# Grouped heads' outputs added on chip, queries stored by halves from ScalarE's queue, latent heads stored by token tiles, in a two-layer grid encoder

## The chip, the cores and the metric

The kernel runs on one core of a Trainium2 chip. The metric is the device time of one execution in microseconds; the time given for a kernel is the median of its runs.

## What is computed

Two request groups, 512 and 256 tokens of width 1024, go through the same two layers and are handled as 768 tokens side by side. Each layer is half an FFN (SwiGLU, inner width 2752), a mixer, half an FFN, with an RMS norm ahead of each. All arithmetic is float32; the kernel gets it from a faster matmul type by splitting operands in a high and a low part and adding the products.

```python
# even layer: the mixer of two head groups
qa, ka, va, cq, ckv, kr = jnp.split(h @ w_in, splits, axis=-1)
oa = _neighbourhood_attention(heads(qa), heads(ka), heads(va), na_bias)   # 8 heads of 64
ob = _mla(cq, ckv, kr, q_norm, w_uq, kv_norm, w_ukv, cos, sin)            # 8 latent heads, 64 + 32
x = x + jnp.concatenate([oa, ob], axis=-1) @ w_out
# odd layer: the grouped mixer, 16 query heads on 4 key/value heads of 64
q = _apply_rope(_rmsnorm(q.reshape(b, n, GQA_HEADS, HEAD_DIM), q_norm), cos, sin)
k = _apply_rope(_rmsnorm(k.reshape(b, n, GQA_KV_HEADS, HEAD_DIM), k_norm), cos, sin)
p = softmax(q k / 8);  o = p v;  x = x + o @ w_out
```

## The kernel before

Features stand on the 128 partitions and tokens along the free axis: `x` is 8 tiles of 128 x 768. Six stages follow one another: FFN, mixer `mixer_ab`, FFN, FFN, mixer `mixer_gqa`, FFN. Inside the FFN stages the order of instructions is the written one (`manual_schedule`); in the mixers the framework's planner places the instructions of each engine by its own estimate of a timeline, under the dependences of tiles and a few added by hand (`anchor`). Each engine, and each DMA queue (SP's and ACT's), then works through its own list in order.

**Attention, shared by both mixers (`attention`, from L1028 on).** A list of heads is worked off in steps. `s_step` makes scores on TensorE (L1079), takes the row maximum on DVE (L1090) and the exponential with its row sum on ACT (L1098); `norm` (L1062, L1065) divides by the sum on DVE and POOL. `t_step` transposes the probabilities on TensorE (L1117) and splits them in a high part `pth` on ACT (L1123) and a low part `ptl` on DVE (L1124). `v_step` multiplies by the values (L1138, L1139); the stationary operand holds the high part of 64 value columns beside their low part, so the output `o` has 128 rows of which the upper and the lower 64 must still be added. `leave` takes `o` out of PSUM, first the 256 tokens of the second group, later the 512 of the first. Between steps, `fill.advance` runs pieces of the projections (`proj`, L944 to L948) and their transposes as filler for TensorE. `poll` is called after each step and moves finished heads on.

**Taking the outputs out.** In `mixer_ab` (`late` false), `leave` copies one half of `o` by ACT (L1162) to `of`, moved to the partitions of the other half, and DVE adds the two (L1163) into `osum`, which holds a pair of heads on 128 partitions. In `mixer_gqa` (`late` true), `leave` copies all 128 rows to `of`, on DVE for 256 tokens (L1160) and on ACT for 512 (L1158), and SP stores them (L1166) in the DRAM scratch `oscr`, where the two halves of a head land as two parts of the same 64 rows.

**From there to the output projection (`out_operand`).** The output projection wants each pair of heads as a high and a low part in the tile `o` (`self.o`). With `bounce` false (`mixer_ab`), `begin` takes the finished `osum` to `split2`: a cast on ACT (L1496) and a subtraction on POOL (L1497); when the filler is not yet over and the tile `o` has no room, `osum` is stored (L1471) and later loaded (L1517). With `bounce` true (`mixer_gqa`), `begin` loads both parts of a pair by SP (L1477); four polls later `split` adds them on POOL (L1484; at the tail on DVE), casts on ACT (L1486, or L1489 while `o` has no room) and subtracts on POOL (L1487, L1490); in the second case the result goes to DRAM (L1491) and comes back later (L1515).

**The grouped queries.** `post_qk` normalizes and rotates four query heads for a pair of token tiles; `later_q` transposes them in two halves of four 128 x 128 blocks (L1865), ACT copies each half into its part of the staging tile `stage` (L1867, one buffer), and SP stores the whole (L1871, 512 KB) in `gq`. A head loads its queries from there (L1893).

**The latent heads.** In `mixer_ab`, `chunk` projects queries and keys of four latent heads for one token tile; `later` transposes them and stages queries (w = 0) and keys (w = 1) apart in `mst` (three buffers), copied half by ACT (L1655) and half by DVE (L1657). SP stores each `mst` (L1659) in `mq`, laid out as 96 rows x (w, head, high/low, 768 tokens). A head reads its 1152 KB from there (L1728; L1550 for the first head), and `kk` and `q` are slices along tokens.

Of the kernel before, what the change touches and what calls it, by code (L numbers as in the profile page):

```python
# [15 lines left out]
P = 128  # L16
# [119 lines left out]
class Kernel:  # L136
# [891 lines left out]
    def attention(self, heads, fill, rate, poll, lead=6, pbufs=9, late=False, start_fill=1400):  # L1028
# [119 lines left out]
        def leave(h, o, moves):  # L1148
# [3 lines left out]
            if not late and k not in sums:  # L1152
                sums[k] = pool.tile([P, T], F32, tag="osum", name="osum", bufs=2)
            for dst, src, w in moves:
                c, sc = slice(dst, dst + w), slice(src, src + w)
                if late:
                    if w > NS:
                        nc.scalar.copy(out=of[:, c], in_=o[:, sc])  # L1158
                    else:
                        nc.vector.tensor_copy(out=of[:, c], in_=o[:, sc])  # L1160
                else:
                    nc.scalar.copy(out=of[mine, c], in_=o[its, sc])  # L1162
                    nc.vector.tensor_tensor(out=sums[k][mine, c], in0=o[mine, sc], in1=of[mine, c], op=ALU.add)  # L1163
            if late:
                a, b = min(m[0] for m in moves), max(m[0] + m[2] for m in moves)
                nc.sync.dma_start(out=self.oscr[k][mine].rearrange("r part t -> part r t")[:, :, a:b], in_=of[:, a:b])  # L1166
# [292 lines left out]
    def out_operand(self, fill, order, bufs, bounce=True):  # L1459
# [5 lines left out]
        S.pool, S.done, S.todo, S.split, S.late, S.polls = None, set(), list(order), deque(), deque(), 0  # L1465

        def begin(k):
            if not bounce:
                t = self.sums.pop(k)
                if S.pool is None:  # L1470
                    nc.sync.dma_start(out=self.oscr[k][:, 0], in_=t)  # L1471
                    S.late.append(k)
                else:
                    split2(k, t)
                return
            t = self.ap_.tile([P, 2, T], F32, tag="osum", name="osum", bufs=bufs)
            nc.sync.dma_start(out=t, in_=self.oscr[k])  # L1477
            S.split.append((S.polls, k, t))

        def split(tail=False):  # L1480
            _, k, t = S.split.popleft()
            eng = nc.vector if tail else nc.gpsimd
            s, r = t[:, 0], t[:, 1]
            eng.tensor_tensor(out=s, in0=s, in1=r, op=ALU.add)  # L1484
            if S.pool is not None:
                nc.scalar.copy(out=self.o[:, k, 1], in_=s)  # L1486
                eng.tensor_tensor(out=self.o[:, k, 0], in0=s, in1=f32(self.o[:, k, 1]), op=ALU.subtract)  # L1487
                return
            nc.scalar.copy(out=r.bitcast(F32R), in_=s)  # L1489
            eng.tensor_tensor(out=s.bitcast(F32R), in0=s, in1=r, op=ALU.subtract)  # L1490
            nc.sync.dma_start(out=self.oscr[k], in_=t)  # L1491
            S.late.append(k)

        def split2(k, t):
# [4 lines left out]
        def poll(slot):  # L1499
# [3 lines left out]
            S.polls += 1  # L1503
            if S.split and S.polls - S.split[0][0] >= 4:
                split()
            elif len(S.split) < bufs and S.todo and {2 * S.todo[0], 2 * S.todo[0] + 1} <= S.done:
                begin(S.todo.pop(0))
# [4 lines left out]
            if S.pool is not None and S.late:  # L1512
                k = S.late.popleft()
                if bounce:
                    nc.sync.dma_start(out=f32(self.o[:, k]), in_=self.oscr[k])  # L1515
                elif k >= 0:
                    nc.sync.dma_start(out=f32(self.o[:, k, 0]), in_=self.oscr[k][:, 0])  # L1517
                    S.late.append(-1 - k)
                else:
                    split2(-1 - k, f32(self.o[:, -1 - k, 0]))  # L1520

        def finish():
            while S.todo or S.split or S.late:
                if S.split:
                    split(True)
                poll(None)
# [555 lines left out]
```

## Time and profile before

| | |
|---|---|
| median of 3 runs | 2880.06 us (2872.93 to 2882.09) |
| the profiled execution | 2872.42 us, span 2870.6 us |
| TensorE, matmuls | 2716.7 us busy, 95% |
| DVE | 1985.3 us, 69% |
| ACT | 1301.5 us, 45% |
| POOL | 292.0 us, 10% |
| moved by DMA | 432.11 MB, mean 151 GB/s |
| mean granted TensorE clock | 0.978 |

All views are of this one execution. Busy times are of the engine, not of its queue: an instruction that issues a DMA isn't counted. The granted clock of a stretch is a mean between 1.00 (2.4 GHz) and 0.50 (1.2 GHz). "A <- B" in the list of waits means that the engine stood idle ahead of A until B was done, with the sum of such times, their number and the longest. Latent heads and their stores lie at about 590 to 700 us, the first mixer's attention at 690 to 895, the grouped attention at 2052 to 2270, its output projection behind it.

### The profile page before, as it was taken

What the parts mean: (1) busy time and instruction counts of PE and PEld (TensorE: products, weight loads), DVE (VectorE), ACT (ScalarE), POOL (GpSimd) and SP (SyncE); (2) the same over time, 40 slices, a digit from 0 to 9 for tenths busy, and PEclk for the clock granted to TensorE, in tenths of its full rate; (3) what the DMA queues carried; (4) which work ended last, traced back from release to release, by engine and by line L of the source; (5) the groups of instructions that cost most, each with busy time, mean ns of one, the idle gap of its engine ahead of it and who ended that gap; (6) DMA issues with size and microseconds to landing.
All of it is one profiled execution on the core that took longest, in us unless ns stands there. A gap on an engine that the chain in (4) does not pass through costs nothing. (4 is left out here: it accounts for less than half of the span.)

```text
span 2870.6 us, 41973 instructions
## 1 busy us (share of the span) xinstructions
PE 2716.7 (95%) x16118; PEld 2646.1 (92%) x16118; DVE 1985.3 (69%) x2902; ACT 1301.5 (45%) x2130; POOL 292.0 (10%) x428
## 2 busy tenths in 40 slices
PE   6999999899989999999999999998987899999998
PEld 6999999898978899999989999998976789999997
DVE  6777678555775676767897676787766467767684
ACT  4443445455675343334444333444566434333443
POOL 0000000032242000000000000002555300000000
PEclk9999999999999999999999999999998999999998
DMA  5474466359874143446544344654334333434752
GB/s 143 121 197 129 131 233 191 121 154 255 265 231 127 59 118 115 123 126 240 177 127 121 109 129 138 222 181 150 96 123 155 139 98 93 125 115 129 250 186 81
DMA packets 415658, 432.11 MB, mean 151 GB/s; under 512 B 34209, under 2 KB 353377, under 8 KB 414433
## 3 DMA queue, kind: packets, MB, share of 16 engines
q1 hardware_dynamic: 401632, 410.55, 47.1%
q10 hardware_dynamic: 13824, 18.88, 1.9%
q8 instruction: 126, 2.06, 0.3%
q14 instruction: 76, 0.61, 0.1%
HBM read 303.60 MB, written 125.76 MB: 150 GB/s over the span
## 5 line engine op out<-in xcount | busy, mean ns | idle before, releaser
L375 ACT CAST guh<-raw 128x1024 fp32r<-128x1024 f32 (+1 forms) x220 | 229.6, 1043 | 300.7 <-DVE raw L517 216.4
L379 DVE TENSOR_TENSOR gul<-raw,guh 128x1024 fp32r<-128x1024 f32 (+1 forms) x220 | 267.4, 1215 | 12.0 <-ACT guh L375 12.0
L477 PE MATMUL y<-tl,guh 128*128 128x384 f32 x696 | 235.3, 338 | 7.1 <-DVE tl L769 6.8
L477 PE MATMUL y<-th,guh 128*128 128x384 f32 x696 | 234.9, 338 | 3.0 <-DVE x L801 3.0
L477 PE MATMUL y<-th,gul 128*128 128x384 f32 x668 | 224.8, 337 | 0.0
L769 DVE TENSOR_TENSOR tl<-traw,th 128x768 fp32r<-128x768 f32 (+1 forms) x156 | 142.6, 914 | 87.9 <-ACT th L767 86.4
L477 PE MATMUL x<-th,guh 128*128 128x384 f32 (+1 forms) x584 | 198.1, 340 | 2.4 <-DVE guh L184 1.8
L477 PE MATMUL x<-tl,guh 128*128 128x384 f32 (+1 forms) x584 | 198.3, 340 | 1.4 <-DVE tl L769 1.1
L641 ACT COPY ap<-ps 128x384 f32<-128x384 f32 x160 | 77.0, 481 | 245.0 <-PE ps L477 244.9
L477 PE MATMUL x<-th,gul 128*128 128x384 f32 (+1 forms) x532 | 179.8, 338 | 0.0
L944 PE MATMUL pj<-guh,h_hi 128*128 128x256 f32 x576 | 169.2, 294 | 0.1
L947 PE MATMUL pj<-gul,h_hi 128*128 128x256 f32 x576 | 165.7, 288 | 2.5 <-DVE gul L189 2.5
L948 PE MATMUL pj<-guh,h_lo 128*128 128x256 f32 x576 | 166.6, 289 | 0.0
L271 POOL TENSOR_TENSOR rc<-ms,expo 128x3 f32<-128x3 f32 (+1 forms) x10 | 10.1, 1012 | 1531.9 <-DVE ms L270 1531.9
L477 PEld LDWEIGHTS y<-tl,guh 128*128 128x128 f32 x696 | 130.6, 188 | 10.2 <-DVE tl L769 10.2
L477 PEld LDWEIGHTS y<-th,guh 128*128 128x128 f32 x696 | 130.6, 188 | 4.4 <-issue 4.2
L767 ACT CAST th<-traw 128x768 fp32r<-128x768 f32 (+1 forms) x156 | 124.2, 796 | 21.5 <-DMA traw<-tq 14.7
L477 PE MATMUL ps<-b11l,guh 128*128 128x384 f32 x368 | 126.2, 343 | 7.3 <-DVE b11l L307 7.3
L1065 POOL TENSOR_SCALAR p<-p,sm 128x256 f32<-128x256 f32 (+1 forms) x192 | 118.4, 628 | 137.1 <-DVE sm L1062 110.2
L647 DVE TENSOR_TENSOR act<-ps,g 128x384 f32<-128x384 f32 x80 | 44.6, 558 | 125.0 <-PE ps L477 119.4
L477 PE MATMUL ps<-o,guh 128*128 128x384 f32 x512 | 131.1, 337 | 0.0
L375 ACT CAST guh<-C 128x1024 fp32r<-128x1024 f32 x60 | 63.1, 1052 | 144.2 <-DVE C L450 96.7
(332 smaller groups left out, 8520.3 us busy)
## 6 DMA issues: line engine op xcount, KB each, us to landing
traw<-tq SPq DMA_DIRECT2D x140, 384.0 KB
raw<-in_ffn_wg_dram SPq DMA_DIRECT2D x84, 512.0 KB
raw<-in_ffn_wd_dram SPq DMA_DIRECT2D x80, 512.0 KB
rawu<-in_ffn_wu_dram SPq DMA_DIRECT2D x76, 512.0 KB
tq<-tl SPq DMA_DIRECT2D x80, 384.0 KB
xscr<-x ACTq DMA_DIRECT2D x96, 192.0 KB
tq<-act SPq DMA_DIRECT2D x40, 384.0 KB
x<-xscr SPq DMA_DIRECT2D x64, 192.0 KB
```

Source lines behind the costliest of these rows:

```text
L271: nc.gpsimd.tensor_tensor(out=self.rc[:, a:b], in0=ms[:, a:b], in1=self.expo[:, a:b], op=ALU.pow)
L375: self.nc.scalar.copy(out=hi, in_=raw)
L379: self.nc.vector.tensor_tensor(out=u[1], in0=raw, in1=f32(u[0]), op=ALU.subtract)
L477: mm = nc.tensor.matmul(out, w, x, start=start and n == 0, stop=stop and n == len(pairs) - 1, skip_group_check=more)
L641: nc.scalar.copy(out=c, in_=ps[:, :TH])
L647: tt(out=act[:, 0], in0=y[:, :TH], in1=g[:, 0], op=ALU.mult)
L767: nc.scalar.copy(out=th[:, :n], in_=t[:, :n])
L769: nc.vector.tensor_tensor(out=tl[:, :n], in0=t[:, :n], in1=f32(th[:, :n]), op=ALU.subtract)
L944: m = nc.tensor.matmul(out, self.h[:, k, s], wh[:, c], start=k == 0, stop=False)
L947: nc.tensor.matmul(out, self.h[:, k, s], wl[:, c], start=False, stop=False)
L948: nc.tensor.matmul(out, self.l[:, k, s], wh[:, c], start=False, stop=k == KT - 1)
L1065: nc.gpsimd.tensor_scalar(out=pt[:, c], in0=pt[:, c], scalar1=sm[:, 2 + s:3 + s], scalar2=1.0, op0=ALU.mult, op1=ALU.mult)
```

## The change

Three things. In both mixers `leave` adds the halves on chip into `osum`, and `out_operand` keeps only the way of `bounce` false; `split2` is now called `split`. In the grouped mixer each half of the staged queries has a tile of its own (two buffers of half the size) and is stored by a DMA from ACT's queue. The latent scratch `mq` is laid out by token tiles, so that what a store writes is one run per partition, and what a head reads is twelve runs per partition (2 x 6 of 1 KB); the slices of `q` and `kk` follow.

```diff
--- before.py
+++ after.py
@@ -1149,21 +1149,12 @@
 
             k, half = divmod(h.slot, 2)
             mine, its = slice(half * HD, half * HD + HD), slice((1 - half) * HD, (1 - half) * HD + HD)
-            if not late and k not in sums:
+            if k not in sums:
                 sums[k] = pool.tile([P, T], F32, tag="osum", name="osum", bufs=2)
             for dst, src, w in moves:
                 c, sc = slice(dst, dst + w), slice(src, src + w)
-                if late:
-                    if w > NS:
-                        nc.scalar.copy(out=of[:, c], in_=o[:, sc])
-                    else:
-                        nc.vector.tensor_copy(out=of[:, c], in_=o[:, sc])
-                else:
-                    nc.scalar.copy(out=of[mine, c], in_=o[its, sc])
-                    nc.vector.tensor_tensor(out=sums[k][mine, c], in0=o[mine, sc], in1=of[mine, c], op=ALU.add)
-            if late:
-                a, b = min(m[0] for m in moves), max(m[0] + m[2] for m in moves)
-                nc.sync.dma_start(out=self.oscr[k][mine].rearrange("r part t -> part r t")[:, :, a:b], in_=of[:, a:b])
+                nc.scalar.copy(out=of[mine, c], in_=o[its, sc])
+                nc.vector.tensor_tensor(out=sums[k][mine, c], in0=o[mine, sc], in1=of[mine, c], op=ALU.add)
 
         start(0)
         for m in range(len(TS)):
@@ -1456,42 +1447,23 @@
             self.rstd_cols(p.tile([P, 512], F32, name="st"))
         self.xpool.close()
 
-    def out_operand(self, fill, order, bufs, bounce=True):
+    def out_operand(self, fill, order):
 
 
         nc = self.nc
         self.ot = ExitStack()
         S = Obj()
-        S.pool, S.done, S.todo, S.split, S.late, S.polls = None, set(), list(order), deque(), deque(), 0
+        S.pool, S.done, S.todo, S.late = None, set(), list(order), deque()
 
         def begin(k):
-            if not bounce:
-                t = self.sums.pop(k)
-                if S.pool is None:
-                    nc.sync.dma_start(out=self.oscr[k][:, 0], in_=t)
-                    S.late.append(k)
-                else:
-                    split2(k, t)
-                return
-            t = self.ap_.tile([P, 2, T], F32, tag="osum", name="osum", bufs=bufs)
-            nc.sync.dma_start(out=t, in_=self.oscr[k])
-            S.split.append((S.polls, k, t))
-
-        def split(tail=False):
-            _, k, t = S.split.popleft()
-            eng = nc.vector if tail else nc.gpsimd
-            s, r = t[:, 0], t[:, 1]
-            eng.tensor_tensor(out=s, in0=s, in1=r, op=ALU.add)
-            if S.pool is not None:
-                nc.scalar.copy(out=self.o[:, k, 1], in_=s)
-                eng.tensor_tensor(out=self.o[:, k, 0], in0=s, in1=f32(self.o[:, k, 1]), op=ALU.subtract)
-                return
-            nc.scalar.copy(out=r.bitcast(F32R), in_=s)
-            eng.tensor_tensor(out=s.bitcast(F32R), in0=s, in1=r, op=ALU.subtract)
-            nc.sync.dma_start(out=self.oscr[k], in_=t)
-            S.late.append(k)
-
-        def split2(k, t):
+            t = self.sums.pop(k)
+            if S.pool is None:
+                nc.sync.dma_start(out=self.oscr[k][:, 0], in_=t)
+                S.late.append(k)
+            else:
+                split(k, t)
+
+        def split(k, t):
             hi, lo = self.o[:, k, 1], self.o[:, k, 0]
             nc.scalar.copy(out=hi, in_=t)
             nc.gpsimd.tensor_tensor(out=lo, in0=t, in1=f32(hi), op=ALU.subtract)
@@ -1500,10 +1472,7 @@
             if slot is not None:
                 S.done.add(slot)
                 return
-            S.polls += 1
-            if S.split and S.polls - S.split[0][0] >= 4:
-                split()
-            elif len(S.split) < bufs and S.todo and {2 * S.todo[0], 2 * S.todo[0] + 1} <= S.done:
+            if S.todo and {2 * S.todo[0], 2 * S.todo[0] + 1} <= S.done:
                 begin(S.todo.pop(0))
             if S.pool is None and fill.over:
                 self.hpool.close()
@@ -1511,18 +1480,14 @@
                 self.o = S.pool.tile([P, KT, 2, T], F32R, name="o")
             if S.pool is not None and S.late:
                 k = S.late.popleft()
-                if bounce:
-                    nc.sync.dma_start(out=f32(self.o[:, k]), in_=self.oscr[k])
-                elif k >= 0:
+                if k >= 0:
                     nc.sync.dma_start(out=f32(self.o[:, k, 0]), in_=self.oscr[k][:, 0])
                     S.late.append(-1 - k)
                 else:
-                    split2(-1 - k, f32(self.o[:, -1 - k, 0]))
+                    split(-1 - k, f32(self.o[:, -1 - k, 0]))
 
         def finish():
-            while S.todo or S.split or S.late:
-                if S.split:
-                    split(True)
+            while S.todo or S.late:
                 poll(None)
         return poll, finish
 
@@ -1546,8 +1511,7 @@
                 yield from self.proj_chunks([[self.post_qk(0)]], 1)
                 for g in range(2):
                     yield from M.chunk(g)
-                M.first = self.qk_tile()[:MD, :4 * T].rearrange("p (w s t) -> p w s t", w=2, s=2)
-                nc.sync.dma_start(out=f32(M.first), in_=M.qk[0][:, :, 0])
+                M.first = self.mla_qk(M, 0)
                 self.anchor = M.ends[4]
                 yield from self.proj_chunks([[self.post_v(0)]], 1)
                 self.anchor = None
@@ -1572,7 +1536,7 @@
                 self.bias = [self.nap.tile([P, 4, 256], F32, name=f"bias{i}") for i in range(2)]
                 for b in self.bias:
                     nc.gpsimd.memset(b, NEG)
-                poll, finish = self.out_operand(fill, order, 1, False)
+                poll, finish = self.out_operand(fill, order)
                 heads = [self.mla_head(M, h) if kind == "m" else self.na_head(h) for kind, h in mix]
                 self.spare_banks = True
                 self.attention(heads, fill, 0.9, poll, start_fill=2100)
@@ -1656,8 +1620,8 @@
                     else:
                         nc.vector.tensor_copy(out=dst, in_=ps[:MD])
                     yield 230
-                nc.sync.dma_start(out=M.qk[g][:, w, :, :, i * P:(i + 1) * P].rearrange("p h s t -> p (h s) t"),
-                                  in_=f32(st).rearrange("p h s t -> p (h s) t"))
+                nc.sync.dma_start(out=M.qk[g][:, w, i].rearrange("p h s t -> p (h s t)"),
+                                  in_=f32(st).rearrange("p h s t -> p (h s t)"))
 
         def product(out, us, n, per, base, count, tok):
             for m in range(count):
@@ -1671,7 +1635,7 @@
         def chunk(g):
             us = [self.gu.get() for _ in range(3)]
             M.v[g] = self.dram.tile([P, 4, TT, 2 * HD], F32, name=f"mv{g}")
-            M.qk[g] = self.dram.tile([MD, 2, 4, 2, T], F32, name=f"mq{g}")
+            M.qk[g] = self.dram.tile([MD, 2, TT, 4, 2, P], F32, name=f"mq{g}")
             for i in range(TT):
                 self.clock += 1
                 self.flip ^= 1
@@ -1714,6 +1678,12 @@
                 self.later(later(g, i, (hq, hk)))
         M.chunk = chunk
 
+    def mla_qk(self, M, h):
+        t = self.qk_tile()[:MD, :4 * T].rearrange("p (w i s t) -> p w i s t", w=2, i=TT, s=2)
+        self.nc.sync.dma_start(out=f32(t).rearrange("p w i s t -> p (w i) (s t)"),
+                               in_=M.qk[h // 4][:, :, :, h % 4].rearrange("p w i s t -> p (w i) (s t)"))
+        return t
+
     def mla_head(self, M, h):
         k, nc = self, self.nc
 
@@ -1724,12 +1694,11 @@
 
             def load(self):
                 if h:
-                    t = k.qk_tile()[:MD, :4 * T].rearrange("p (w s t) -> p w s t", w=2, s=2)
-                    nc.sync.dma_start(out=f32(t), in_=M.qk[h // 4][:, :, h % 4])
+                    t = k.mla_qk(M, h)
                 else:
                     t = M.first
-                q = lambda a: [t[:, 0, s, a:a + P] for s in (0, 0, 1)]
-                kk = lambda a, e: [t[:, 1, s, a:e] for s in (0, 1, 0)]
+                q = lambda a: [t[:, 0, a // P, s] for s in (0, 0, 1)]
+                kk = lambda a, e: [t[:, 1, a // P:e // P, s] for s in (0, 1, 0)]
                 k.dense_steps(self, q, kk, 1.0)
 
             def load_v(self):
@@ -1857,18 +1826,18 @@
                             yield 230
 
                 def later_q(pair, hl):
-                    stage = S.gp.tile([P, 4, 256], F32R, tag="stage", name="stage", bufs=1)
                     for half in range(2):
+                        stage = S.gp.tile([P, 2, 256], F32R, tag="stage", name="stage", bufs=2)
                         ps = self.tq_bank()
                         for b in range(4):
                             hd, t = 2 * half + b // 2, b % 2
                             nc.tensor.transpose(ps[:, b * P:(b + 1) * P].bitcast(F32R),
                                                 hl[:, t, hd].rearrange("p s d -> p (s d)"), self.identr)
-                        nc.scalar.copy(out=stage[:, 2 * half:2 * half + 2], in_=ps.rearrange("p (h t) -> p h t", h=2))
+                        nc.scalar.copy(out=stage, in_=ps.rearrange("p (h t) -> p h t", h=2))
+                        nc.scalar.dma_start(out=S.q[c][:, 2 * half:2 * half + 2, 256 * pair:256 * pair + 256], in_=f32(stage))
                         if half:
                             self.held -= 1
                         yield 230
-                    nc.sync.dma_start(out=S.q[c][:, :, 256 * pair:256 * pair + 256], in_=f32(stage))
                 return post
 
             def gen():
@@ -1901,7 +1870,7 @@
                     def v(self, i):
                         return S.v[:, i, h // 4].rearrange("p s d -> p (s d)")
                 return Head()
-            poll, finish = self.out_operand(fill, order, 1)
+            poll, finish = self.out_operand(fill, order)
             self.spare_banks = False
             self.attention([head(h) for h in range(GH)], fill, 0.7, poll, late=True)
             fill.drain()
```

## Rows read from the trace of the kernel before

**Rows 1.** Windows: length; busy PE, PEld, DVE, ACT, POOL; clock; DMA share; GB/s.
```profile
2060.00:2187.00 127.00, 101.38 (x677) 89.68 (x676) 86.19 (x175) 77.95 (x185) 79.15 (x91) 0.91 0.46 146
2187.00:2270.00 83.00, 69.79 (x360) 54.74 (x360) 56.01 (x126) 57.44 (x147) 41.87 (x53) 0.89 0.33 112
590.00:720.00 130.00, 120.77 (x895) 113.23 (x894) 64.64 (x115) 67.59 (x137) 36.16 (x82) 0.95 0.80 223
720.00:900.00 180.00, 166.90 (x1199) 153.80 (x1198) 133.81 (x279) 128.12 (x323) 65.68 (x107) 0.96 0.71 214
```
**Rows 2.** Waits of PE, 2100 to 2190 us: sum, times, longest.
```profile
PE t L1117 <- ACT p L1098: 6.5, 2, 6.1
PE o L1138 <- ACT pth L1123: 5.8, 1, 5.8
PE tq L1865 <- ACT stage L1867: 5.6, 1, 5.6
PE s L1079 <- ACT stage L1867: 3.7, 1, 3.7
```

**Rows 3.** Waits of ACT, then of POOL, 2060 to 2300 us.
```profile
ACT osum L1489 <- POOL osum L1484: 13.9, 2, 7.1
...
POOL osum L1484 <- DMA osum<-oscr: 49.2, 7, 9.0
```

**Rows 4.** Windows over one wait of each kind, and the stretch behind the first.
```profile
2111.90:2118.00 6.10, 0.28 (x5) 0.14 (x3) 0.05 (x1) 1.40 (x3) 3.20 (x4) 0.93 0.44 172
2118.00:2126.00 8.00, 7.90 (x37) 6.99 (x38) 5.16 (x11) 5.56 (x13) 7.76 (x9) 0.62 0.38 123
2167.30:2174.40 7.10, 0.98 (x7) 0.66 (x6) 2.52 (x5) 2.13 (x5) 2.95 (x4) 0.82 0.90 297
```

**Rows 5.** Waits of PE, 2190 to 2275 us.
```profile
PE t L1117 <- POOL p L1065: 6.6, 4, 2.6
```

**Rows 6.** Timeline of ACT, the long output copies: start, duration (of nine, three).
```profile
2195.31 0.60 ACT L1158 COPY of<-o 128x512 f32<-128x512 f32 x1
2203.87 0.59 ACT L1158 COPY of<-o 128x512 f32<-128x512 f32 x1 [0.51 <-DMA oscr<-of]
...
2275.25 0.59 ACT L1158 COPY of<-o 128x512 f32<-128x512 f32 x1 [2.06 <-DMA oscr<-of]
```

**Rows 7.** Instructions on the tile `of`: ns min/median/max, first and last start, forms.
```profile
L1162 ACT COPY of<-o x40: 204/370/587, 722.5 to 894.1; 64x256 f32<-64x256 f32 x16, 64x512 f32<-64x512 f32 x8, 64x448 f32<-64x448 f32 x8, 64x64 f32<-64x64 f32 x8
L1163 DVE TENSOR_TENSOR osum<-o,of x40: 197/428/695, 722.9 to 894.7; 64x256 f32<-64x256 f32 x16, 64x512 f32<-64x512 f32 x8, 64x448 f32<-64x448 f32 x8, 64x64 f32<-64x64 f32 x8
...
L1160 DVE COPY of<-o x16: 406/425/426, 2078.4 to 2268.3; 128x256 f32<-128x256 f32 x16
L1158 ACT COPY of<-o x16: 576/588/637, 2085.8 to 2275.3; 128x512 f32<-128x512 f32 x16
```

**Rows 8.** DMA issues on the tiles `gq` and `xscr`: ns min/median/max.
```profile
L1893 SPq DMA_DIRECT2D gq<-gq x16: 320/414/5621, 2019.5 to 2238.8; - x16
L1871 SPq DMA_DIRECT2D gq<-stage x12: 513/554/3605, 2003.5 to 2187.1; - x12
...
L292 ACTq DMA_DIRECT2D xscr<-x x96: 326/327/1511, 33.4 to 2341.9; - x96
```

**Rows 9.** Waits of PE, 590 to 720 us.
```profile
PE gt L1652 <- ACT mst L1655: 7.1, 7, 2.2
...
PE gt L1652 <- DVE mst L1657: 0.7, 1, 0.7
```

**Rows 10.** Windows over the latent stores and behind the grouped attention, as rows 1.
```profile
2280.00:2300.00 20.00, 20.00 (x117) 20.00 (x116) 9.14 (x13) 5.90 (x9) 0.00 (x0) 1.00 0.75 279
620.00:700.00 80.00, 70.77 (x511) 64.80 (x510) 40.64 (x72) 40.04 (x85) 19.71 (x46) 0.91 0.97 268
```

**Rows 11.** Waits of PE, 720 to 900 us.
```profile
PE s L1079 <- DMA qk<-mq: 4.9, 2, 3.1
...
PE o L1138 <- DVE osum L1163: 0.6, 1, 0.6
```

## The prediction

> **What bounds the kernel now.** I read the page first: TensorE is busy 95% of the span, so time can only come out of places where it stands or runs at half clock. The windows over the stages show three such places inside the stages that the change touches. The grouped attention splits at 2187 us into a stretch that still has projections to fill gaps and one that has not. In the first, 127 us long, TensorE is busy 101.4 us and idle 25.6; in the second, 83 us long, it is idle 13.2. The latent stage (590 to 720 us) has 9.2 us idle in 130 [rows 1]. The granted clock in the same rows is 0.91, 0.89 and 0.95: between the levels 2.4 and 1.2 GHz that is 2 x 0.09 x 127 = 23, 18 and 13 us at the lower one.
>
> The waits say what ends the idle times. In the first stretch four waits make 21.6 us of the 25.6: two on ACT (6.1 of the 6.5 and all of the 5.8 us) and two on the query staging copy (5.6 and 3.7) [rows 2]. The first two lie one step further back. ACT stands 13.9 us, twice, in front of the cast at L1489, which waits for POOL's add of the two output parts, and POOL stands 49.2 us over seven such adds for the reload of these parts from DRAM [rows 3]. Since ACT works in order, exponentials that TensorE needs are queued behind that cast. The windows show it once: 2111.9 to 2118.0 has TensorE busy 0.28 us, and the 8 us behind it run at clock 0.62 [rows 4]. In the second stretch POOL, standing at the same reload, holds the normalizations behind it: 6.6 us in four waits [rows 5].
>
> **The grouped outputs.** Removed for 16 heads: 32 stores, 8 reloads of 768 KB, 8 adds of parts (seven on POOL, the last on DVE), and for the two pairs finished early a store and reload of both halves (one half stays). The stalls that go: 11.9 us in the first stretch with no successor, because the new cast waits only for an add already queued ahead of it on DVE. In the second stretch I go by the rhythm of heads. The long output copies start at 2195.31, 2203.87, ..., 2275.25: eight heads in 79.94 us, 10.0 each, while an undisturbed one took 8.56 [rows 6]. That bounds the gain there at 8 x 1.44 = 11.5 us; the idle time plus half of the time at low clock (13.2 + 9) is the other end, 22. I take 11.5, the nearer thing to a measured rhythm.
>
> Added per head: ACT copies 64 rows twice instead of 128 once, 0.370 + 0.587 for 0.588 us, so 0.37 more; DVE adds 0.428 + 0.695 for a copy of 0.425, so 0.70 more [rows 7]. (The medians 0.370 and 0.428 stand for the 256 columns, the maxima for 512.) DVE is busy 86 of 127 and 56 of 83 us, ACT 78 and 57 [rows 1], so this is not all hidden once the stalls are gone. I count half of the larger, 0.35 us, for 15 heads: 5 us, with 0 and 11 as ends. The DVE add also waits in order behind ACT's copy. In the first mixer, which already adds its outputs on chip, TensorE waited 0.6 us for that add in the whole attention [rows 11]; I cost it at nothing.
>
> **The query stores.** A pair of token tiles is staged in one buffer and stored by SP; now each half has its own buffer and its store leaves from ACT. What the stall at 2167.3 to 2174.4 shows is a late landing: the DMA engines are 0.90 busy there at 297 GB/s [rows 4], and SP's own issues, median 0.55 and 0.41 us, took up to 3.6 and 5.6 [rows 8]. With the reloads gone that crowd thins, the half store needs one staging copy and not two, and it stands behind nothing on SP. So I take the 9.3 us [rows 2] as gone. The price is 24 issues on ACT. The same engine issues the stores of x at 0.327 us median, 1.511 at most [rows 8]: 7.8 us, ends 0 and 36. ACT is busy 78 of 127 us, so I count half on the path, 4 us.
>
> The clock comes back with the stalls. Of the 23 us at 1.2 GHz in the first stretch each costs half a microsecond of matmul work, 11.5 in all; part lies in idle time, so I take 8.
>
> First stretch: 11.9 + 9.3 + 8 - 4 = 25. Second: 11.5. Less 5 for the added copies: 31.5 us for the grouped part.
>
> **The latent stores.** Each of 24 stores now writes one row of 4 KB per partition and not eight of 512 B. TensorE waits 7.8 us there for the staging copies [rows 9], whose buffers are held by stores under way. From 620 to 700 us the DMA engines are 0.97 busy and move 268 GB/s; at 2280 they moved 279 GB/s at 0.75 busy, which is 372 at full [rows 10]. The 24 stores are 9.4 MB, so at 372 for 268 they free 35 - 25 = 10 us of engine time in a stage with 16 us to win (9.2 idle, 6.5 of clock). I take 7, ends 0 and 16. The heads read back worse: 1 KB pieces instead of 6 KB. A head's 1.18 MB takes 3.2 us at 372 and 4.4 at 268 GB/s, 1.2 more. Loads go out a head ahead, yet two of them already hold TensorE, 4.9 us in all [rows 11], so I count those two: 2.4, ends 0 and 9.6 for all eight.
>
> The Trainium skill (DMA: Bandwidth & Descriptors, Specifications) gives 512 B as the least transfer for line rate. By that rule the new rows gain nothing and the sum is 7 us smaller; the two rates of rows 10 speak against it, though their mix of loads and stores differs.
>
> **The sum.** 31.5 + 7 - 2.4 = 36 us. The profiled execution ran 2872.4 us (span 2870.6), 7.7 under the median of 2880.1; so 2836 for it and 2844 for a median.
>
> **Rivals.**
> *The store lands as late.* Everything still runs through the same 16 DMA engines, so the staging buffer is held as long. The staging stalls stay, 9.3 plus some 3 us of clock, and ACT now pays its issues in full (4 more): 36 - 16 = 20 us, 2860. For it speaks the DMA share of 0.90 in the stall [rows 4]; against it that most of that traffic is the reload that goes. The Trainium skill (DMA: Bandwidth & Descriptors, Issuing engines are not separate DMA queues) says that issuing from several engines only saves issue time on the sequencer, and names this outcome as far as the queue goes.
>
> *The order moves.* In both attentions the planner places instructions by its own estimates; new edges give a new order, and stalls as large as the removed ones appear elsewhere. Against it: the first mixer keeps 0.96 of the clock and 93% busy with the same on-chip adds [rows 1]. Price: the whole gain, 2880.
>
> *ACT's queue is held by the stores (slower).* Place: the first stretch, between staging copy and exponentials. If the queue pushes back as it did on SP, an issue costs up to 3.6 us [rows 8], and every exponential behind it waits. With nothing hidden it decides from (36 + 4) / 24 = 1.7 us each; at 2.5 us it is 60 us against 40, so 2900. For it: one issue of 1.51 on ACT. Against it: the median 0.327 over 96 of them, and less traffic than now.
>
> **How the numbers follow.** Forecast 0.62, late landing 0.18, new order 0.10, ACT held 0.10. About 0.3%, 9 us, is what a measurement can tell here. The forecast's own range is 2812 (gains at their upper ends, 11.5 + 11 + 9 more than taken) to 2855 (latent part nothing, added copies in full). Late landing reaches to 2870. The range 2812 to 2870 leaves out 0.2. Faster 0.80, same 0.10, slower 0.10.
>
> **What would show it.** Right: no load of output parts in grouped attention; no ACT wait on a POOL add; POOL's longest waits there not on DMA; eight late heads at about 9 us each; clock above 0.95 from 2060 on; in the latent stage the staging wait under 3 us and a DMA share clearly under 0.97. Late landing: ACT's staging copy still waits for its store. ACT held: stores from ACT over 1 us each with exponentials late behind them. The forecast is wrong if DVE or ACT fills the freed time, seen as matmuls that wait on output adds or on exponentials in every head.

## The result, and the profile after

The changed kernel takes 2836.82 us in the median of 4 runs (2832.7 to 2840.79) against 2878.36 of the kernel before: the ratio is 0.9854, with a 95% interval of 0.9836 to 0.9871, so 41.5 us less. The forecast was 2844 (36 less), range 2812 to 2870. Run once more beside another kernel it took 2842.95 against 2877.1, ratio 0.9881 (0.9863 to 0.99). Between the two profiles of the changed kernel the stages that the change touches agree within 0.3 us; the rest lies outside them: 3.6 us ahead of the first mixer, 2.9 between the mixers, 6.2 behind the first output projection matmul. Differences of a few us between single runs are therefore read below from the stages, not from the end.

Three marks do that: the first projection of the first mixer, the first matmul of the output projections, and the first grouped score. From the first grouped score to the first output projection matmul it is 216.8 us before (2052.9 to 2269.7) and 177.6 after (2057.1 to 2234.7): 39.2 us, all but 2 of the total. The first mixer, from its first projection to its output projection, is 310.0 before and 309.8 after.

The stretch can be parted once more. ACT copies the 512 tokens of the first group out for each of the 16 heads; the eighth of these long copies is the first behind the last query store. Up to it, it is 142.4 us before (2052.9 to 2195.3) and 119.6 after (2057.1 to 2176.7), 22.8 less; from there to the output projection 74.4 and 58.0, 16.4 less.

The windows over this stretch, split where the projections end, first of the kernel before (length; busy PE, PEld, DVE, ACT, POOL; clock; DMA share; GB/s):

```profile
2053.00:2147.00 94.00, 86.06 (x619) 78.51 (x618) 72.38 (x143) 62.63 (x146) 62.51 (x71) 0.96 0.38 117
2147.00:2269.70 122.70, 91.81 (x474) 72.44 (x473) 75.10 (x166) 78.53 (x195) 63.32 (x78) 0.86 0.42 138
```

and of the changed one:

```profile
2057.00:2142.00 85.00, 83.47 (x619) 77.52 (x618) 73.85 (x146) 66.75 (x155) 62.01 (x72) 0.98 0.33 100
2142.00:2234.70 92.70, 81.63 (x476) 64.00 (x475) 84.42 (x179) 83.22 (x205) 57.46 (x72) 0.98 0.24 72
```

TensorE runs as many matmuls (1093 and 1095). Its idle time fell from 38.8 to 12.6 us, and the same number of matmuls takes 165.1 us in place of 177.9, at a granted clock of 0.98 in place of 0.96 and 0.86. So 26 us of the 39 are standing time, and 13 are matmuls that run faster at that clock.

The waits of PE after, from 2050 to 2160 and from 2160 to 2240 us, answer to [rows 2] and [rows 5]:

```profile
PE t L1117 <- DVE sm L1062: 1.4, 2, 1.1
PE o L1138 <- DVE osum L1157: 1.2, 1, 1.2
...
PE s L1079 <- ACT p L1098: 2.4, 7, 0.7
PE o L1139 <- DVE ptl L1124: 1.7, 6, 0.4
```

None is over 1.5 us at a time: no staging copy, no normalization on POOL. ACT's list has no wait on a POOL add any more, and POOL's largest sum is for DVE's reciprocals, not for a reload [rows 3] (from 2050 to 2240 us):

```profile
POOL p L1065 <- DVE sm L1062: 35.7, 29, 3.1
POOL o L1469 <- ACT o L1468: 10.1, 5, 6.4
```

The rhythm of the late heads is read as in [rows 6], by the last eight intervals of ACT's long copies: 58.1 us from 2176.74 to 2234.86, 7.3 a head, where it was 79.9 us and 10.0:

```profile
2176.74 0.58 ACT L1156 COPY of<-o 64x512 f32<-64x512 f32 x1
...
2190.69 0.58 ACT L1156 COPY of<-o 64x512 f32<-64x512 f32 x1 [0.59 <-PE o L1139]
...
2234.86 0.58 ACT L1156 COPY of<-o 64x512 f32<-64x512 f32 x1 [1.63 <-PE o L1139]
```

The kernels below that add on chip and copy as the change does (e1, e3, e5, e7, e13) take 58.1 to 58.2 us for the same eight. In a window over these heads three engines are busy 64 to 65 of 70 us, TensorE, DVE and ACT, with TensorE at full clock:

```profile
2160.00:2230.00 70.00, 63.60 (x379) 50.49 (x377) 64.06 (x141) 64.66 (x163) 41.69 (x57) 1.00 0.18 50
```

The latent stage moved little. Waits of PE from 590 to 720 us, which answer to [rows 9]:

```profile
PE gt L1616 <- ACT mst L1619: 6.0, 5, 1.9
...
PE gt L1616 <- DVE mst L1621: 0.7, 1, 0.7
```

The staging copies hold TensorE 6.7 us where it was 7.8. The window that answers to [rows 10]:

```profile
620.00:700.00 80.00, 70.60 (x530) 65.00 (x529) 42.28 (x77) 41.17 (x86) 20.86 (x48) 0.94 0.93 277
```

### The profile page after: what moved, and what is told of

Read it like the earlier page. It is cut to its first block, busy times and chain, and to the rows that moved or that the text cites. A ratio compares the mean times of both kernels' runs of the same rounds, so it can differ in the third digit from the quotient of the medians.

```text
span 2830.7 us, 41923 instructions
## 1 busy us (share of the span) xinstructions
PE 2703.9 (96%) x16118; PEld 2638.0 (93%) x16118; DVE 1994.1 (70%) x2916; ACT 1309.0 (46%) x2146; POOL 283.4 (10%) x422
## 5 line engine op out<-in xcount | busy, mean ns | idle before, releaser
L477 PE MATMUL ps<-b11l,guh 128*128 128x384 f32 x368 | 126.0, 342 | 7.2 <-DVE b11l L307 7.2
```

The source lines that it names most:

```text
L477: mm = nc.tensor.matmul(out, w, x, start=start and n == 0, stop=stop and n == len(pairs) - 1, skip_group_check=more)
```

## The experiments

A letter stands for the theory or rival that the expectation of that run describes. Times are medians; "before" is the kernel before on the same chip.

| run | us | before | ratio, 95% interval |
|---|---|---|---|
| e1 grouped part only | 2835.28 | 2878.09 | 0.9854, 0.9837 to 0.987 |
| e2 latent layout only | 2874.31 | 2878.09 | 0.9986, 0.9975 to 0.9997 |
| e3 outputs only | 2837.32 | 2878.09 | 0.986, 0.9845 to 0.9875 |
| e4 query stores only | 2887.49 | 2878.09 | 1.003, 1.0019 to 1.004 |
| e5 change, half stores from SP | 2834.01 | 2876.84 | 0.985, 0.9836 to 0.9865 |
| e7 change, half the latent bytes | 2831.45 | 2878.15 | 0.9839, 0.9825 to 0.9852 |
| e8 change, halves not added | 2834.59 | 2878.15 | 0.9846, 0.9832 to 0.9859 |
| e9 DRAM, add put off | 2880.61 | 2878.15 | 1.0003, 0.9993 to 1.0013 |
| e10 half stores from SP only | 2873.21 | 2878.15 | 0.9988, 0.9978 to 0.9999 |
| e11 DRAM, reload and add put off | 2864.82 | 2876.84 | 0.9961, 0.995 to 0.9973 |
| e12 change, work moved to POOL | 2840.92 | 2877.1 | 0.9877, 0.9857 to 0.9897 |
| e13 the change again | 2842.95 | 2877.1 | 0.9881, 0.9863 to 0.99 |

**The outputs alone.** The kernel before with `leave` and `out_operand` of the change, whole; queries and latent scratch as before.

```diff
-            if late:
...
-                nc.sync.dma_start(out=self.oscr[k][mine].rearrange("r part t -> part r t")[:, :, a:b], in_=of[:, a:b])
+                nc.scalar.copy(out=of[mine, c], in_=o[its, sc])
+                nc.vector.tensor_tensor(out=sums[k][mine, c], in0=o[mine, sc], in1=of[mine, c], op=ALU.add)
...
-            t = self.ap_.tile([P, 2, T], F32, tag="osum", name="osum", bufs=bufs)
-            nc.sync.dma_start(out=t, in_=self.oscr[k])
-            S.split.append((S.polls, k, t))
+            t = self.sums.pop(k)
```

> The kernel before with the grouped outputs added on chip, queries still staged whole and stored from SP, old latent layout. Theory A (outputs and query stores each remove their own stalls): 2844 to 2848 us, so 30 to 34 under before, and the staging copy still waits 4 to 9 us for its store. Rival B (the query store was late only because of the output traffic): 2837 us like the whole change, and the staging copy no longer waits.

It is the whole gain, 40.8 us: 2837.3, and 176.1 us from the first grouped score to the output projection. The staging copy, whose single buffer and SP store were left as they were, no longer waits. On the tile `stage`, the wait of its writers for the store that had to land (us, times), of the kernel before:

```profile
  DMA gq<-stage: 9.6, 2
```

and of this kernel, with the store above it (ns min/median/max of an issue, first and last start):

```profile
L1836 SPq DMA_DIRECT2D gq<-stage x12: 513/519/582, 2010.9 to 2171.3; - x12
...
  DMA gq<-stage: 0.3, 1
```

The longest issue of this store is 0.58 us where it was 3.6 [rows 8], and 0.3 us is all that the copies wait for it. Rival B holds: the stores were late because of the outputs' way through DRAM, and the 9.3 us at the staging copy belonged to it. Whether the traffic or SP's queue made them late is not told apart here.

**The queries alone**, on the kernel before, from ACT and from SP.

```diff
-                    stage = S.gp.tile([P, 4, 256], ..., bufs=1)     # ahead of the loop over halves
+                    stage = S.gp.tile([P, 2, 256], ..., bufs=2)     # in it, and a store in it:
+                    nc.scalar.dma_start(out=S.q[c][:, 2 * half:2 * half + 2, ...], in_=f32(stage))   # e10: nc.sync
```

> The kernel before with the queries stored by halves from ACT alone; outputs still go through DRAM. Theory A: 2866 to 2870 us, 8 to 12 under before, no wait of the staging copy on its store, ACT still stands at POOL's adds for 25 us or more. Rival B: 2875 us or more, the staging copy still waits for its store since the output traffic is there.

> The kernel before with the queries staged and stored by halves, but from SP. Theory Q (the issues on ACT cost the 9 us that the stores from ACT alone lost): 2875 to 2880 us. Rival B (ACT's issue costs next to nothing; halving moves the order, and the stall moves to another place behind the output traffic): 2884 to 2890 us as with ACT.

From ACT it is 9.4 us slower, from SP 4.9 faster. So on the kernel before it is the queue, and not the halving, that loses time: rival B of e10, which had 2884 to 2890 us, is out, and theory Q's range is missed by 1.8 us only. That the issues themselves cost the 9 us, as Q says, is not shown. They are short and even, on the tile `gq` in e4:

```profile
L1868 ACTq DMA_DIRECT2D gq<-stage x24: 366/366/400, 2007.1 to 2187.2; - x24
```

24 x 0.366 is 8.8 us, and 14.3 us lie between the two versions. In the profiles most of the difference lies behind the last of these stores: from the first grouped score to the eighth long output copy e4 takes 140.4 us and e10 138.5, from there to the output projection 81.8 and 77.4. (As wholes these two profiles lie only 5.2 us apart; that of e4 is the fastest of its runs.) It shows in matmuls that wait for exponentials, 14.1 us against 7.4 from 2160 to 2275 us, and 7.7 against 0.7 from 2190 us on. Waits of PE from 2160 us on, of e4:

```profile
PE s L1079 <- ACT p L1098: 12.5, 4, 6.1
...
PE t L1117 <- ACT p L1098: 1.6, 2, 1.3
```

and of e10:

```profile
PE t L1117 <- ACT p L1098: 7.2, 3, 4.9
...
PE s L1079 <- ACT p L1098: 0.2, 1, 0.2
```

ACT makes the exponentials. From 2050 to 2300 us it stands at POOL's adds as long in all three kernels (before 32.1 us, e4 34.0, e10 34.6), so that does not tell them apart; for its output buffer it stands 5.6 us before, 16.0 in e4 and 5.0 in e10. Why the buffer comes free later in e4 stays open. The staging copy of e4 waits for its store no more, as A said, yet TensorE still stands 5.7 us at one staging copy.

**The queue in the changed kernel.** One word of the change, `nc.scalar.dma_start` to `nc.sync.dma_start`.

> The whole change, but the half stores of the queries leave from SP. Theory Q (an issue on ACT costs some 0.6 us of the path, as the two query versions without the output change differ by 14 us over 24 issues): 2825 to 2831 us. Rival B (with the output traffic gone neither queue is in anyone's way): 2834 to 2839 us.

2834.0 us is the lower end of rival B's range; theory Q's 0.6 us an issue is out. The stretch tells it better: with stores from ACT 177.6, 177.8 (e13) and 177.4 us (e1), from SP 175.9 (e5) and 176.1 (e3). Issued from ACT, the stores cost some 1.6 us here.

**What it is in the way through DRAM.** Two versions of the kernel before that keep the way and only wait later.

```diff
-            if S.split and S.polls - S.split[0][0] >= 4:
+            if S.split and S.polls - S.split[0][0] >= 9:      # e11: 6, and begin() five polls after the pair
...
-            eng.tensor_tensor(out=s, in0=s, in1=r, op=ALU.add)
+            first = eng.tensor_tensor(out=s, in0=s, in1=r, op=ALU.add)
+            if self.anchor is not None:
+                self.tc.add_manual_dep(first.ins, self.anchor.name, NOSYNC, reason="late")   # e11: the reload too
```

> The kernel before, outputs still through DRAM, but POOL's add of the two parts comes nine polls after the reload and not four, and is placed behind the matmuls of that moment. Theory A (what cost time is that ACT and POOL stand, in order, at a reload that lands later than the planner's estimate): ACT waits on POOL's adds under 8 us (32 before), 2845 to 2858 us. Rival D (the traffic itself costs, through late stores and loads): over 2868 us, with other waits on DMA in their place.

> The kernel before, outputs through DRAM, with the reload issued five polls after a pair is done and POOL's add six polls after that, both placed behind the matmuls of that moment. Theory H (with the add put off, the loss moved to the output buffer, because SP stands in order at the reload until the pair's stores have landed, and later stores wait behind it): ACT and DVE wait for stores of output copies under 15 us together (39.9 with the add alone put off, 14.3 before), 2850 to 2866 us. Rival D (the way through DRAM costs what it costs, through its traffic and its one buffer): these waits stay over 25 us or others on DMA take their place, 2872 us or more.

By end time e9 gains nothing. ACT's standing at POOL's adds fell in it from 32.1 us to 8.7 and the stretch stayed at 216.7. More waiting shows at the output copies instead, which may not overwrite their one buffer before its store has landed. Waits of ACT and DVE, 2060 to 2300 us, of the kernel before:

```profile
ACT o L1486 <- POOL osum L1484: 18.2, 4, 5.1
...
ACT of L1158 <- DMA oscr<-of: 5.6, 6, 2.1
...
DVE of L1160 <- DMA oscr<-of: 8.7, 4, 3.0
```

and, from 2050 us, of e9:

```profile
ACT of L1158 <- DMA oscr<-of: 17.0, 6, 6.4
...
ACT o L1488 <- POOL osum L1484: 8.7, 2, 5.0
...
DVE of L1160 <- DMA oscr<-of: 22.9, 8, 5.0
```

With the reload put off as well (e11) the stretch is 198.6 us, 18 less than before, and the output projection behind it is 7 us longer (from its first to its last matmul 2260.0 to 2336.0, 76.0 us against 68.7): TensorE stands 2.8 us there for the cast of a late pair, and the granted clock is 0.94 in place of 1.00. Its time is what H expected, its waits are not: they stay at 35.1 us.

```profile
ACT of L1158 <- DMA oscr<-of: 14.9, 5, 5.3
...
DVE of L1160 <- DMA oscr<-of: 20.2, 8, 6.7
```

What did fall is the time that SP stands at the reload until the pair's stores have landed, first before (39.5 us in e9), then in e11:

```profile
SPq L1477 <- DMA oscr<-of: 43.0, 9, 7.7
...
SPq L1477 <- DMA oscr<-of: 18.8, 4, 7.1
```

So neither theory holds whole. Of the 39 us, 18 in the stretch could be had by waiting later; whether the other 21 hang on the one output buffer, on the traffic or on the order is not shown. A second output buffer, which would tell the buffer from the traffic, was not tried.

**What the adds cost.** The change with `nc.vector.tensor_copy(out=sums[k][mine, c], in_=o[mine, sc])` for the copy and the add in the grouped mixer; half of each output is left out.

> The whole change, but in the grouped mixer the halves are not added: DVE copies the half of the high parts, ACT's copy of the other half and the add are left out (so the low part of the values is missing from the output). Theory A (once the stalls are gone DVE and ACT, 19 of 20 us busy, set the late heads): 0.4 to 0.9 us less per head, 2826 to 2831 us. Rival E (the added work lies beside matmuls): 2835 to 2838 us.

The stretch is 175.3 us, 2.3 less, all of it in the late heads, about 0.3 us each. ACT is relieved (56 of 70 us), DVE is as busy as before, since its copy takes as long as its add (0.550 and 0.545 us in the median):

```profile
2155.00:2225.00 70.00, 64.05 (x391) 51.72 (x389) 64.91 (x143) 56.42 (x146) 43.91 (x60) 1.00 0.18 50
```

By end time rival E is nearer. What DVE's longer work costs is not measured by this run, which leaves that work in place. So work was moved from DVE and ACT to POOL (with the half stores from SP, as in e5).

```diff
+                if late and w == NS:
+                    nc.scalar.copy(out=sums[k][mine, c], in_=o[mine, sc])
+                    nc.gpsimd.tensor_tensor(out=sums[k][mine, c], in0=sums[k][mine, c], in1=of[mine, c], op=ALU.add)
+                    continue
...
-            nc.scalar.copy(out=hi, in_=t)
+            nc.gpsimd.tensor_scalar(out=hi, in0=t, scalar1=1.0, scalar2=1.0, op0=ALU.mult, op1=ALU.mult)   # grouped mixer
```

> The whole change with half query stores from SP, and in the grouped mixer two pieces of work moved to POOL: for the 256 tokens of the second group ACT copies both halves and POOL adds them, and POOL makes the cast to the high part. Per head DVE loses 0.43 us, ACT 0.05, POOL gains about 1.6. Theory I (DVE, 64 of 70 us busy, sets the late heads): 3 to 6 us less than the changed kernel on the same chip. Rival J (the heads are set by the chain through all engines, and POOL's longer work delays the normalizations behind it): no gain or a loss of up to 10 us, with matmuls waiting on POOL's normalization.

> The changed kernel itself, as the measure for the run beside it: 2833 to 2840 us, in every theory.

2.0 us less than the change beside it, inside the spread, and the stretch is longer: 185.0 us against 175.9 in e5. Most of that lies up to the eighth long copy (126.0 us against 118.0). The late heads behind it take 59.3 us for eight intervals, no less than the 58.1 of the change, though DVE has less to do. The window from 2160 us on, which begins ahead of the eighth copy:

```profile
2160.00:2230.00 70.00, 61.25 (x345) 48.78 (x345) 58.74 (x127) 59.51 (x154) 47.21 (x67) 0.93 0.15 42
```

DVE is busy 58.7 us in place of 64.1, and theory I's 3 to 6 us did not come. The time is rival J's, but its sign did not come: of all waits of TensorE in the stretch 0.4 us are for POOL's normalization, and 2.2 for the cast that was moved to POOL. Whether POOL's added work hides a gain on DVE stays open, and with it whether any one engine sets the late heads.

**The latent layout**, alone (e2), and left out (e1). e2 takes these lines of the change and the loads that go with them:

```diff
-                nc.sync.dma_start(out=M.qk[g][:, w, :, :, i * P:(i + 1) * P].rearrange("p h s t -> p (h s) t"),
+                nc.sync.dma_start(out=M.qk[g][:, w, i].rearrange("p h s t -> p (h s t)"),
...
-            M.qk[g] = self.dram.tile([MD, 2, 4, 2, T], F32, name=f"mq{g}")
+            M.qk[g] = self.dram.tile([MD, 2, TT, 4, 2, P], F32, name=f"mq{g}")
```

> The kernel before with the new layout alone. Theory A: 2878 us within 4, matmul waits on the staging copies between 6 and 8 us, DMA share from 620 to 700 us still over 0.90. Rival C: 2872 to 2874 us, waits clearly under 5 us.

> The change without the new layout of the latent scratch. Theory A (the layout is worth nothing, the grouped part carries all): 2837 us, 41 under the kernel before, the first mixer's output projection starts at 894 us as with the whole change. Rival C (the layout is worth the 4.6 us forecast and one profile hides it): 2841 to 2843 us.

By the end times the two disagree (3.8 us with an interval from 0.9 to 7.2; nothing). e2 stands between its theories: its time is at the edge of both, its waits on the staging copies, 4.7 us, are C's, its DMA share of 0.93 is A's. The stages of all profiles say more. From the first projection of the first mixer to its output projection, six profiles with the new layout (the change, e13, e2, e5, e8, e12) take 306.4 to 309.8, mean 307.7; seven without it (before, e1, e3, e4, e9, e10, e11) take 310.0 to 313.4, mean 310.9. So the layout gives about 3 us in the mean, and little in the two profiles of the change itself (309.8 and 309.7). The waits of TensorE on the staging copies fall as much, from 7.8 to 10.7 us (mean 9.0) without the layout to 4.7 to 7.0 (mean 5.9) with it. The first score comes 4 us earlier; about 1 is given back.

The last run halves the bytes of these stores: `M.qk[g][:, w, i, :2]` from `st[:, :2]`, and heads read slot `h % 2`.

> The whole change, but each latent store writes two of its four heads (half the bytes; heads 2, 3, 6 and 7 then read the queries and keys of heads 0, 1, 4 and 5). Theory F (bytes through the DMA engines bind the latent stage, whatever the row length): matmul waits on the staging copies under 3 us, 2829 to 2833 us. Rival G (the fixed time from issue to landing or SP's queue holds the buffers): waits 5 us or more, 2835 to 2838 us.

The stage is 303.5 us, 4 less again than the mean with the new layout. The staging copies wait 4.1 us for stores where the change waits 27.0, and TensorE waits 4.5 us (4.2 and 0.3) for the staging copies. The window reads:

```profile
620.00:700.00 80.00, 74.21 (x580) 68.84 (x579) 45.17 (x84) 43.36 (x92) 21.63 (x49) 0.98 0.80 232
```

The time is F's, the waits lie between. Half the bytes at the same number of rows are worth 4 us, an eighth of the rows at the same bytes 3. And with the waits for stores nearly gone, TensorE's waits for staging copies are hardly under those of e2 (4.7): not all of them hang on the stores. The traffic of 620 to 700 us, first of the kernel before,

```profile
DMA packets 34034, 21.40 MB, mean 268 GB/s; under 512 B 908, under 2 KB 33599, under 8 KB 34027
```

and of the changed one,

```profile
DMA packets 21095, 22.18 MB, mean 277 GB/s; under 512 B 937, under 2 KB 18666, under 8 KB 21088
```

has 38% fewer packets and a DMA share that went from 0.97 to 0.93 only. At full that is 276 and 298 GB/s for all that moves there, of which the stores in question are 9 of 22 MB.

## Why the prediction was right, and where its terms were not

**The sum** was 36 us and came out at 41 and 34. Its terms did worse than it, and that it is near is in part luck: a stall was priced rightly and put to the wrong edit of the same change, and one term that was too large stands beside one that was too small. (In the working, the four waits named in the first stretch add to 21.2 us; 21.6 are the five of [rows 2]. And the first 11.5 us of the lower bound is not worked out anywhere.)

**The grouped outputs, 11.9 + 11.5 - 5 with 8 for the clock: right in kind, too small.** The chain of ACT behind POOL behind the reload was what the rows said, and it is gone. Two sizes were off. The staging stalls, put to the query stores, are the outputs', too: e3 measures 40.8 us for the outputs where the terms without the staging give 26. And the late heads, which were to take about 9 us each and take 7.3, gained 16.4 us where 11.5 less their share of the added copies was counted. The 8.56 us that the prediction took for an undisturbed head was one of the shortest intervals of a disturbed kernel, and its own row shows 0.51 us of waiting for a store [rows 6]. By the rhythm that it went by, eight heads went from 79.9 to 58.1 us, 21.8 less and so at the upper end of the term, 22, with the added copies in it.

**The added copies, 5.** No run measures this term whole. With ACT's copies of the other half left out (e8) the stretch is 2.3 us shorter; DVE's part stays in that run. The wait for an output add, costed at nothing, is 1.2 us, once.

**The query stores, 9.3 - 4: wrong.** The row (DMA engines 0.90 busy in the stall) was read rightly, the credit went to the wrong edit: e3 leaves the stores as they were and the stall is gone, e4 changes only them and the kernel is slower. With the outputs on chip there was nothing left to win, and leaving from ACT cost 1.6 us. The rule of the Trainium skill behind the late-landing rival (DMA: Bandwidth & Descriptors, Issuing engines are not separate DMA queues), that another issuing engine saves only issue time, agrees: the stretch takes 175.9 us with the stores from SP and 177.6 with them from ACT. The rival's premise, a store that lands as late, did not come.

**ACT held by the stores** did not come in the changed kernel: an issue took 0.366 us in the median and 0.797 at most, where the rival needed 1.7. On the kernel before, e4 shows the late exponentials that it foretold and 9.4 us lost. But no issue took over 0.400 us there, and in the profile most of the loss lies behind the last of them, so the price was another and the mechanism is not shown.

**The clock** gave 13 us over the whole stretch, where 8 were counted for its first part.

**The latent part, 7 - 2.4: 3 measured, near by net.** The term that was mis-sized is the engine time that longer rows set free: 372 GB/s from a stretch mostly of loads was put to the 9.4 MB of stores, which gave 10 us. From 620 to 700 us all traffic went from 276 to 298 GB/s at full. The 22.18 MB of that window take 80 us of engine time at the one rate and 74 at the other, so an estimate of what was set free is 6 us. What the Trainium skill (DMA: Bandwidth & Descriptors, Specifications) says, that 512 B is the least transfer for line rate, was argued against in the prediction; the 6 us stand between the nothing of that rule and the prediction's 10. The staging wait was to fall under 3 us and stayed at 6.7; e7 shows that not all of it was the stores'. The 2.4 us for reads in smaller pieces show in no run: TensorE waits 6.6 us for these loads in the change and 4.9 before [rows 11], but 0.2 to 7.0 over the six profiles with the new layout and 4.9 to 7.4 over the seven without.

**The order** brought no stall of the removed size into the grouped attention of the changed kernel: no wait of TensorE there is over 1.5 us (in e13 one is 2.1, for an output add).

## What to carry to other kernels

When several late transfers stand in one trace, ask whose traffic they stand behind before giving each its own remedy: here 9.3 of 36 us were put to an edit that was worth nothing once another was made. A wait put off in an ordered queue may come back at the next buffer (14.3 us there became 39.9 in e9), so see first whether the round trip itself can go. The shortest interval of a disturbed kernel is not yet an undisturbed one. And a DMA rate taken from a stretch mostly of loads was too high for stores.

## What the runs showed of the hardware

An issue of a store on ACT took 0.366 us in the median. 24 of them, issued from ACT and not from SP, made the stretch 1.6 us longer where the outputs were added on chip; where they went through DRAM, the part of the stretch in which the stores leave was 2.0 us longer (140.4 and 138.5 us), in one profile each. The 14.3 us between the medians of those two kernels are not explained by the issues. Rows of 4 KB in place of 512 B, in the stores that make 9 of 22 MB of the traffic, raised what the 16 DMA engines moved at full from 276 to 298 GB/s; over all profiles it is 273 to 279 with the old rows and 295 to 301 with the new.
